# Causal attention from the last tokens to the first, with the mask added to the gate rows on GpSimd

## The chip, the cores and the metric

The kernel runs on one core of one Trainium2 chip. The metric is the device time of one execution in microseconds (us). TensorE (PE) multiplies matrices, VectorE (DVE) and ScalarE (ACT) work on whole tiles, GpSimd (POOL) does some elementwise work and issues some DMAs, SyncE (SP) issues most DMAs. The engines run their own instruction lists in order and wait for each other by semaphores.

## What is computed

One decoder layer on 1024 tokens of width 1024: a projection into four pooling groups and 8 heads of attention with a forget gate, an output projection with layer norm, and an MLP of width 4096 with layer norm. The part that matters here:

```python
log_f = log_sigmoid(f_logit); cf = cumsum(log_f)          # per head
s = (q @ k.T) * HEAD_DIM ** -0.5
s = s + cf[:, None] - cf[None, :]
s = where(kpos <= qpos, s, NEG_INF)                       # causal
p = softmax(s); out = p @ v
x = layer_norm(ALPHA * x + concat([pool_out, out]) @ w_out)
```

The term `cf` of the query drops out of the softmax, so the kernel only adds `-cf` of the keys.

## The kernel before, in words

Matrices are split into a high and a low part (`split`, L70 to L72), and a product takes three passes of TensorE (`three`, L83 to L85). In order of time the program projects values and gates, then three of the four pooling groups, then queries and keys of head pair 0, then runs attention, the output projection with the first norm (from L725, in four pieces `m` of 256 tokens), and the MLP.

Attention (L318 to L443) goes over head pairs `p`, heads `e` of a pair, and pieces `m` of 256 query tokens; one (p, e, m) is a unit. Pairs 0 to 2 run one head after the other with m = 0, 1, 2, 3; pair 3 alternates its two heads for each m. A unit has two halves.

- `att_probs`: for each of its two blocks `i` of 128 queries, and for each piece of up to 512 keys up to the diagonal, two passes give scores in a PSUM bank with the tag "s" (three such banks; L339, L340). If the piece holds the diagonal, a third pass (L342) adds the causal mask, a bf16 identity against a bf16 mask of 128x128. Then DVE's L345 adds the head's gate row, turns the sign and keeps the running minimum, which is the query's maximum; ACT's L347 takes the exponential and the row sum.
- `att_values`: for each 256 keys TensorE transposes the probabilities into a "pt" bank (L368), ACT copies the high part (L369), DVE makes the low part (L370), and TensorE multiplies with the values (L384). The last such tile has a quarter set to zero by POOL (L366). ACT and DVE put the two halves of the result together (L389, L390), and SP writes it to `mix_dram` (L391). `row_scales` turns the row sums into factors (L399 to L404).

The gate row of a head is a line of `ncf_dram` sent to all 128 partitions (L326), into one of the nine buffers of tag "A", where the probabilities and the turned tiles live too. It is asked for by the head's first unit.

`att_values` of a unit is written after `att_probs` of the next one. In between, `fillstep` doles out pieces of other work for TensorE: in pairs 0 to 2 the projection of the next pair's keys and queries (`qk_proj`, 33 pieces over 28 steps), in pair 3 the last pooling group (`pool_group` and `pool_linear`, L242 to L280, 18 pieces over 14 steps). What is left of the pieces runs at the pair's end. A scheduler then sets the order on each engine from this text. The buffers of the token tiles come free as the last pooling group has used them, and take the weights of the output projection, which are split on ACT and DVE inside pair 3.

```python
        prob = att_probs(*unit)
        ...
        fillstep()
        if pend is not None:
            att_values(*pend)
        pend = (*unit, prob)
    run(gen)
```

Of the kernel before, what the change touches and what calls it, by code (L numbers as in the profile page):

```python
# [36 lines left out]
def trunk(ctx, tc, xT, xn, wuqk, wvf, bf, poolw, pscale, wout, g1, b1, w1, w2, g2, b2, out):  # L37
# [13 lines left out]
    def slot(tag, shape, dt=F32R):  # L51
        uid[0] += 1
        return sb.tile([P] + list(shape), dt, tag=tag, bufs=NBUF[tag], name=f"{tag}{uid[0]}")

    def small(shape, tag, dt=F32, bufs=1, pool=None):
        uid[0] += 1
        return (pool or sb).tile(list(shape), dt, tag=tag, bufs=bufs, name=f"{tag}_{uid[0]}")
# [29 lines left out]

    ident = small([P, P], "ident")
    make_identity(nc, ident)
    identb = small([P, P], "identb", BF16)  # L90
    nc.vector.tensor_copy(identb, ident)
    maskb = small([P, P], "maskb", BF16)
    nc.gpsimd.memset(maskb, 0.0)
    nc.gpsimd.affine_select(
        out=maskb, in_=maskb, pattern=[[-1, P]], compare_op=ALU.is_ge,
# [140 lines left out]
    def run(gen):  # L236
        for _ in gen:
            pass
# [51 lines left out]
    def qk_proj(p, tag=None):  # L290
        KS, Q1, Q2 = zip(*([slot("Q", [S]) for _ in range(3)] for _ in range(2)))
        QK[p] = (KS, Q1, Q2)
        lo_, hi_ = slice(0, HD), slice(HD, P)
        w = load_w(wuqk[2 * NPAIR + p])
        for c in range(NCH):
            cs = slice(c * CH, (c + 1) * CH)
            kp = bank(tag)
            for _ in proj(kp, c, w):
                yield
            nc.scalar.copy(KS[0][lo_, cs], kp[lo_])  # L300
            nc.scalar.copy(KS[1][hi_, cs], kp[hi_])
            nc.vector.tensor_tensor(KS[0][hi_, cs], kp[lo_], KS[0][lo_, cs].bitcast(F32), ALU.subtract)
            nc.vector.tensor_tensor(KS[1][lo_, cs], kp[hi_], KS[1][hi_, cs].bitcast(F32), ALU.subtract)
        w = load_w(wuqk[NPAIR + p])
        sc = HD ** -0.5
        for c in range(NCH):
            cs = slice(c * CH, (c + 1) * CH)
            qp = bank(tag)
            for _ in proj(qp, c, w):
                yield  # L310
            for e, r in ((0, lo_), (1, hi_)):
                nc.scalar.mul(Q1[e][r, cs], qp[r], sc)
                nc.vector.scalar_tensor_tensor(Q2[e][r, cs], qp[r], sc, Q1[e][r, cs].bitcast(F32), ALU.mult, ALU.subtract)
            for e, r, o in ((0, lo_, hi_), (1, hi_, lo_)):
                nc.vector.tensor_copy(Q1[e][o, cs], Q1[e][r, cs].bitcast(F32))
                nc.vector.tensor_copy(Q2[e][o, cs], Q2[e][r, cs].bitcast(F32))

    gate_rows, rsum = {}, {}  # L318

    def att_probs(p, e, m):  # L320
        KS, Q1, Q2 = (part[e] for part in QK[p])
        h = 2 * p + e
        if h not in gate_rows:
            gate_rows[h] = slot("A", [S], F32)
            rsum[h] = small([P, NT], "rsum", bufs=3)
            nc.sync.dma_start(gate_rows[h], ncf_dram[h : h + 1, :].to_broadcast([P, S]))  # L326
        nb = gate_rows[h]
        prob = []
        for i in (2 * m, 2 * m + 1):
            nk = (i + 1) * P  # L330
            n2 = nk if m % 2 else 256 * (m + 1)
            qs = slice(i * P, (i + 1) * P)
            pt = slot("A", [S], F32)
            top = BIG
            for a in range(0, nk, CH):
                b = min(n2, a + CH)
                diag = a <= i * P < b
                sp = bank("s")[:, : b - a]
                nc.tensor.matmul(sp, Q1[:, qs], KS[:, a:b], start=True, stop=False)  # L339
                nc.tensor.matmul(sp, Q2[:, qs], KS[:, a:b], start=False, stop=not diag)  # L340
                if diag:
                    nc.tensor.matmul(sp[:, i * P - a : (i + 1) * P - a], identb, maskb, start=False, stop=True)  # L342
                b = min(nk, b)
                nm = small([P, 1], "nm", bufs=8)
                nc.vector.tensor_tensor_reduce(pt[:, a:b], sp[:, : b - a], nb[:, a:b], -1.0, top, ALU.add, ALU.min, nm)  # L345
                top = nm
            nc.scalar.activation(pt[:, :nk], pt[:, :nk], AF.Exp, bias=nm, scale=-1.0, accum_out=rsum[h][:, i : i + 1])  # L347
            prob.append(pt)
        return prob

    def att_values(p, e, m, prob):
        h = 2 * p + e
        rows = slice(e * HD, (e + 1) * HD)
        orow = slice((1 - e) * HD, (2 - e) * HD)
        ov = bank("pv")[:, 0:256]

        def turned(jp):
            tp = bank("pt")
            tt = slot("A", [2, CH])
            if jp < m:  # L360
                blocks = [(jj * 256 + ii * P, 2 * jp + jj, ii) for jj in range(2) for ii in range(2)]
                ev = slice(0, CH)
            else:
                blocks = [(P, 2 * jp + 1, 1), (2 * P, 2 * jp, 0), (3 * P, 2 * jp, 1)]
                ev = slice(P, CH)
                nc.gpsimd.memset(tt[:, :, 0:P].bitcast(F32), 0.0)  # L366
            for col, j, ii in blocks:
                nc.tensor.transpose(tp[:, col : col + P], prob[ii][:, j * P : (j + 1) * P], ident)  # L368
            nc.scalar.copy(tt[:, 0, ev], tp[:, ev])  # L369
            nc.vector.tensor_tensor(tt[:, 1, ev], tp[:, ev], tt[:, 0, ev].bitcast(F32), ALU.subtract)  # L370
            return tt

        nxt = turned(0)
        for jp in range(m + 1):
            tt = nxt
            if jp < m:
                nxt = turned(jp + 1)
            fillstep()
            mov = ((0, 256), (256, CH)) if jp < m else ((256, CH), (0, 256))
            for s in range(2):  # L380
                for jj in range(2):
                    j = 2 * jp + jj
                    a, b = mov[jj]
                    nc.tensor.matmul(  # L384
                        ov, V[j][:, h].rearrange("p s d -> p (s d)"), tt[:, s, a:b],
                        start=(j == 0 and s == 0), stop=(j == 2 * m + 1 and s == 1),
                    )
        mx = slot("U", [256], F32)
        nc.scalar.copy(mx[rows], ov[orow])  # L389
        nc.vector.tensor_tensor(mx[rows], ov[rows], mx[rows], ALU.add)  # L390
        nc.sync.dma_start(mix_dram[m, rows, NG + p, :], mx[rows])  # L391
        if p == NPAIR - 1:
            row_scales(h, 2 * m, 2)
        elif m == 3:
            row_scales(h, 0, NT)

    def row_scales(h, i, n):
        ri = small([P, NT], "ri", bufs=2)
        nc.vector.reciprocal(ri[:, :n], rsum[h][:, i : i + n])  # L399
        tp = bank("pt")  # L400
        nc.tensor.transpose(tp[0:n, 0:P], ri[:, :n], ident)
        row = small([NT, P], "row")
        nc.scalar.copy(row[0:n], tp[0:n, 0:P])
        nc.sync.dma_start(rin_dram[h, i * P : (i + n) * P].rearrange("(i q) -> i q", q=P), row[0:n])  # L404
# [14 lines left out]
    def fillstep():  # L419
        fill["credit"] += fill["rate"]  # L420
        while fill["credit"] >= 1.0:
            fill["credit"] -= 1.0
            next(fill["gen"], None)

    pend = None
    for p in range(NPAIR):
        if p + 1 < NPAIR:
            order = [(p, e, m) for e in range(2) for m in range(4)]
            gen, pieces, over = qk_proj(p + 1, "mm"), 4 * KT + 1, 28
        else:  # L430
            order = [(p, e, m) for m in range(4) for e in range(2)]
            gen, pieces, over = last_fill(), (2 * KT + 2) * len(LATE), 14
        fill.update(gen=gen, credit=0.0, rate=pieces / over)
        for unit in order:
            prob = att_probs(*unit)
            if pend is None:
                for g in EARLY[1:]:
                    pool_linear(g, "A")
            fillstep()
            if pend is not None:  # L440
                att_values(*pend)
            pend = (*unit, prob)
        run(gen)  # L443
    att_values(*pend)


# [275 lines left out]
    NU = NF // 2  # L722
    units = [Unit(u) for u in range(NU)]
    last = None
    for m in range(4):  # L725
        mh = []
        for half in range(2):
            mf = slot("S", [4, 256], F32)
# [7 lines left out]
            hi, lo = slot("Q", [4, 256]), slot("Q", [4, 256])  # L736
            split(hi, lo, mf)
            mh.append((hi, lo))
        for t in (2 * m, 2 * m + 1):
            ts_ = slice((t % 2) * P, (t % 2 + 1) * P)  # L740
            xt = slot("A", [D], F32)
            nc.sync.dma_start(xt, xn[t])
            if t == NT - 1:
                for un in units[:2]:
                    un.load_f()
# [146 lines left out]
    class Step:  # L892
# [61 lines left out]
        def p1(self):  # L954
            self.k1 = bank("s")
            self.prod(self.k1, "A11", "B11", True)
            self.into(0, c0, self.k1, True)
            if self.final:
                self.n0, self.n1 = (Norm(y[t], *rows["gb"], out[t]) for t in (self.q, self.q + 4))

        def p2(self):

# [159 lines left out]
```

## Time and profile before

| | |
|---|---|
| median of 3 runs | 1051.55 us (1051.01 to 1051.81) |
| the profiled execution, its own time | 1053.88 us |
| its span in the profile | 1052.1 us |
| busy: PE, DVE, ACT, POOL | 1021.7, 757.9, 513.1, 116.1 us |
| mask passes (L342) | 64 |
| bytes by DMA | 195.81 MB |

"Busy" is time in which an engine has an instruction at work. Matmuls overlap, so the duration of one is longer than the time between two starts; for what a pass costs, starts are compared. The time in brackets behind a row is how long the engine had been idle before it, with what ended the wait.

### The profile page before, as it was taken

The page shows a single profiled execution, that of the slowest core. Times are in us where ns is not written, and L with a number is a line of the kernel's source. Part 1 is how long each engine was busy: PE and PEld are TensorE (multiplying, and loading weights), DVE is VectorE, ACT ScalarE, POOL GpSimd, SP SyncE. Part 2 cuts the span into 40 slices and gives each one's busy share as a digit, 9 for nine tenths or more (in the row PEclk, how much of TensorE's full clock was granted, in tenths as well). Part 3 has the DMA queues.
Part 4 walks back from the last instruction along what each step waited for, and adds up shares of the span by engine and source line. Part 5 has one row for each costly group of instructions (what it writes and reads, how often), then busy time and mean ns, then how long its engine had stood idle before and what let it go on. Part 6 is the DMA issues. An engine that isn't in the chain of part 4 may idle for free.

```text
span 1052.1 us, 14040 instructions
## 1 busy us (share of the span) xinstructions
PE 1021.7 (97%) x5006; PEld 845.7 (80%) x5006; DVE 757.9 (72%) x1297; ACT 513.1 (49%) x822; POOL 116.1 (11%) x187
## 2 busy tenths in 40 slices
PE   8999999999989999999999999999999999999994
PEld 8988787888777878887888888888788888888883
DVE  4576678686785896989887878788876665566346
ACT  4423565565774331676666766768521212222153
POOL 0000000000000021112112122120100000000056
PEclk9999999999999999999999999999999999999998
DMA  6302311111345633139756667565999888868753
GB/s 221 104 27 93 113 51 32 31 53 50 115 145 169 200 131 110 61 112 349 295 224 266 234 248 271 221 259 195 345 311 300 284 266 279 274 200 276 228 183 120
DMA packets 111654, 195.81 MB, mean 186 GB/s; under 512 B 9240, under 2 KB 77656, under 8 KB 111584
## 3 DMA queue, kind: packets, MB, share of 16 engines
q1 hardware_dynamic: 95600, 136.71, 39.7%
q0 software_dynamic: 15984, 58.20, 14.3%
q8 instruction: 39, 0.64, 0.3%
q14 instruction: 31, 0.25, 0.1%
HBM read 127.18 MB, written 67.70 MB: 185 GB/s over the span
## 4 chain that ended last, share of the span: by engine, by line
PE 52%; DVE 4%; DMA 2%; issue 1%; ACT 0%; DVEq 0%; SPq 0%; ACTq 0%
PE s L932 15%; PE s L578 9%; PE pv L932 8%; PE pt L578 6%; PE mm L578 6%; PE pv L578 4%; PE pt L932 2%; PE mm L932 2%; DMA S<-in_w_dram 1%; DVE B L72 1%; DMA A<-hid_dram 1%; DVE A L701 0%; DVE Q L72 0%; DVE A L516 0%; ACT Q L71 0%
## 5 line engine op out<-in xcount | busy, mean ns | idle before, releaser
L71 ACT CAST B<-S 128x1024 fp32r<-128x1024 f32 (+1 forms) x92 | 78.5, 870 | 178.4 <-DMA S<-in_w_dram 66.5
L72 DVE TENSOR_TENSOR B<-S,B 128x1024 fp32r<-128x1024 f32 (+1 forms) x92 | 90.4, 994 | 39.4 <-ACT B L71 39.1
L578 PE MATMUL s<-B,Q 128*128 128x512 f32 x480 | 113.5, 389 | 0.1
L578 PEld LDWEIGHTS s<-B,Q 128*128 128x128 f32 x480 | 90.0, 188 | 19.2 <-ACT B L71 0.5
L932 PE MATMUL s<-B,Q 128*128 128x512 f32 x399 | 97.2, 390 | 0.0
L932 PEld LDWEIGHTS s<-B,Q 128*128 128x128 f32 x399 | 74.9, 188 | 16.0
L932 PE MATMUL s<-B,A 128*128 128x512 f32 x333 | 83.0, 394 | 3.7 <-DVE rt L499 2.2
L71 ACT CAST Q<-S 128x1024 fp32r<-128x1024 f32 x52 | 54.6, 1050 | 64.3 <-PE s L578 17.0
L932 PEld LDWEIGHTS s<-B,A 128*128 128x128 f32 x333 | 62.3, 188 | 18.9 <-DVE rt L499 2.6
L72 DVE TENSOR_TENSOR Q<-S,Q 128x1024 fp32r<-128x1024 f32 x52 | 63.3, 1216 | 13.8 <-ACT Q L71 13.7
L703 POOL DMA_DIRECT2D hid_dram<-A x90 | 48.2, 540 | 219.6 <-ACT A L700 174.6
L578 PE MATMUL pt<-B,Q 128*128 128x512 f32 x300 | 71.6, 389 | 0.0
L578 PE MATMUL mm<-B,Q 128*128 128x512 f32 x300 | 71.6, 389 | 0.0
L384 PE MATMUL pv<-A,B 128*128 128x256 f32 x320 | 61.9, 298 | 4.8 <-ACT A L369 3.3
L384 PEld LDWEIGHTS pv<-A,B 128*128 128x128 f32 x320 | 49.4, 189 | 21.1 <-ACT A L369 9.7
L578 PEld LDWEIGHTS pt<-B,Q 128*128 128x128 f32 x300 | 56.3, 188 | 11.7
L578 PEld LDWEIGHTS mm<-B,Q 128*128 128x128 f32 x300 | 56.3, 188 | 11.7
L370 DVE TENSOR_TENSOR A<-pt,A 128x512 fp32r<-128x512 f32 (+1 forms) x80 | 49.2, 634 | 16.3 <-ACT A L369 15.7
L347 ACT ACTIVATE A<-A,nm 128x128 f32<-128x128 f32 (+3 forms) x64 | 49.8, 778 | 22.2 <-DVE nm L345 21.9
L701 DVE TENSOR_TENSOR A<-A,A 128x1024 f32<-128x1024 f32 x45 | 53.6, 1219 | 0.0
L83 PE MATMUL mm<-B,B 128*128 128x512 f32 x120 | 51.7, 431 | 0.0
L932 PE MATMUL pv<-B,Q 128*128 128x512 f32 x204 | 50.3, 390 | 0.0
(399 smaller groups left out, 2263.0 us busy)
## 6 DMA issues: line engine op xcount, KB each, us to landing
hid_dram<-A POOLq DMA_DIRECT2D x105, 512.0 KB, 3.9
S<-in_w_dram SPq DMA_DIRECT2D x62, 512.0 KB
Q<-hid_dram SPq DMA_DIRECT2D x104, 256.0 KB
A<-hid_dram SPq DMA_DIRECT2D x76, 256.0 KB
S<-in_wuqk_dram SPq DMA_DIRECT2D x12, 512.0 KB
A<-ncf_dram SPq DMA_DIRECT2D x8, 512.0 KB
S<-in_wout_dram SPq DMA_DIRECT2D x8, 512.0 KB
S<-mix_dram SPq DMA_DIRECT2D x8, 512.0 KB
```

Source lines behind the costliest of these rows:

```text
L71: nc.scalar.copy(hi, src)
L72: nc.vector.tensor_tensor(lo, src, hi.bitcast(F32), ALU.subtract)
L83: nc.tensor.matmul(dst, a[0], b[0], start=first, stop=False)
L347: nc.scalar.activation(pt[:, :nk], pt[:, :nk], AF.Exp, bias=nm, scale=-1.0, accum_out=rsum[h][:, i : i + 1])
L370: nc.vector.tensor_tensor(tt[:, 1, ev], tp[:, ev], tt[:, 0, ev].bitcast(F32), ALU.subtract)
L384: nc.tensor.matmul(ov, V[j][:, h].rearrange("p s d -> p (s d)"), tt[:, s, a:b], start=(j == 0 and s == 0), stop=(j == 2 * m + 1 and s == 1),)
L578: nc.tensor.matmul(dst, b[x][:, k], A[a][y][:, k], start=first and k == 0 and i == 0, stop=k == H - 1 and i == 2, skip_group_check=not first,)
L701: nc.vector.tensor_tensor(x, x, hi.bitcast(F32), ALU.subtract)
L703: nc.gpsimd.dma_start(hid_dram[self.u, :, i, AT[name] : AT[name] + 2 * CH], part.rearrange("p q n t -> p (q n t)"))
L932: nc.tensor.matmul(dst, h[:, p_], w[q_], start=first and u == self.us[0] and j == 0, stop=u == self.us[-1] and j == 2, skip_group_check=no ...
```

## The change

The units run with m = 3, 2, 1, 0, and in each unit the upper block comes first. Before a block's scores, POOL adds the mask, now a float tile, to the 128 columns of the gate row that belong to the block, in place. The blocks above have used these columns without it, and the blocks below don't read them. The mask pass of TensorE, the bf16 identity and its copy go. The gate row of the next unit's head is asked for right after `att_probs` of the current unit. In `qk_proj` the second half of the queries is made first. The output projection takes its four pieces in the order 3, 2, 1, 0, and `PLACE` sends rows to their places in the input and output.

```diff
-    identb = small([P, P], "identb", BF16)
-    nc.vector.tensor_copy(identb, ident)
-    maskb = small([P, P], "maskb", BF16)
+    maskb = small([P, P], "maskb")
...
-        for c in range(NCH):
+        for c in reversed(range(NCH)):
...
+    def gate_row(h):
         if h not in gate_rows:
             gate_rows[h] = slot("A", [S], F32)
             rsum[h] = small([P, NT], "rsum", bufs=3)
             nc.sync.dma_start(gate_rows[h], ncf_dram[h : h + 1, :].to_broadcast([P, S]))
...
-        for i in (2 * m, 2 * m + 1):
+        for i in (2 * m + 1, 2 * m):
             nk = (i + 1) * P
             n2 = nk if m % 2 else 256 * (m + 1)
             qs = slice(i * P, (i + 1) * P)
+            nc.gpsimd.tensor_tensor(nb[:, qs], nb[:, qs], maskb, ALU.add)
...
-                diag = a <= i * P < b
                 sp = bank("s")[:, : b - a]
                 nc.tensor.matmul(sp, Q1[:, qs], KS[:, a:b], start=True, stop=False)
-                nc.tensor.matmul(sp, Q2[:, qs], KS[:, a:b], start=False, stop=not diag)
-                if diag:
-                    nc.tensor.matmul(sp[:, i * P - a : (i + 1) * P - a], identb, maskb, start=False, stop=True)
+                nc.tensor.matmul(sp, Q2[:, qs], KS[:, a:b], start=False, stop=True)
...
-        elif m == 3:
+        elif m == 0:
             row_scales(h, 0, NT)
+    PLACE = [6, 7, 4, 5, 2, 3, 0, 1]
...
+    order = [(p, e, m) for p in range(NPAIR - 1) for e in range(2) for m in (3, 2, 1, 0)]
+    order += [(NPAIR - 1, e, m) for m in (3, 2, 1, 0) for e in range(2)]
...
+        prob = att_probs(*unit)
+        if n + 1 < len(order):
+            gate_row(2 * order[n + 1][0] + order[n + 1][1])
...
-    for m in range(4):
+    for n in range(4):
+        m = 3 - n
...
-            nc.sync.dma_start(xt, xn[t])
+            nc.sync.dma_start(xt, xn[PLACE[t]])
...
-                self.n0, self.n1 = (Norm(y[t], *rows["gb"], out[t]) for t in (self.q, self.q + 4))
+                self.n0, self.n1 = (Norm(y[t], *rows["gb"], out[PLACE[t]]) for t in (self.q, self.q + 4))
```

The order of instructions moves in many places. Three of them follow; the lines of the changed kernel lie a few numbers off (L342 and L343 are there the two score passes, L346 the reduce, L371 the low part of a turned tile, L322 the load of a gate row). The first is TensorE at the start of pair 3, before:

```order
L339 MATMUL s_2876<-Q_2283,Q_2284 128x256
L340 MATMUL s_2876<-Q_2283,Q_2285 128x256
L342 LDWEIGHTS identb_68
L342 MATMUL s_2876<-maskb_70,identb_68 128x128
L339 MATMUL s_2884<-Q_2283,Q_2284 128x256
```

and now:

```order
L342 MATMUL s_2911<-Q_2327,Q_2328 128x512
L343 MATMUL s_2911<-Q_2327,Q_2329 128x512
L342 MATMUL s_2916<-Q_2327,Q_2328 128x512
L343 MATMUL s_2916<-Q_2327,Q_2329 128x512
L342 MATMUL s_2924<-Q_2327,Q_2328 128x512
```

The unit of the first 256 tokens with its two small blocks has made way for the last 256 tokens, whose block takes two banks, and the weight load and the pass of the mask are gone.

The second is VectorE in pair 2, at the two reduces of the unit m = 1 of head 4 (blocks 2 and 3; A_2264 and A_2252 are the gate row), before:

```order
L345 ISA A_2370,nm_2375<-s_2371,A_2264 128x384 [waits DVE_49,PE_49]
L345 ISA nm_2375 128x1
L370 TENSOR_TENSOR A_2323<-pt_2322,A_2323 128x512 [waits Activation_49]
L345 ISA A_2378,nm_2383<-s_2379,A_2264 128x512 [waits DVE_49,PE_49]
L345 ISA nm_2383 128x1
```

and now:

```order
L346 ISA A_2467,nm_2471<-s_2468,A_2252 128x512 [waits DVE_49,PE_49,Pool_49]
L346 ISA nm_2471 128x1
L371 TENSOR_TENSOR A_2423<-pt_2422,A_2423 128x512 [waits Activation_49]
L346 ISA A_2475,nm_2479<-s_2476,A_2252 128x384 [waits PE_49,Pool_49]
L346 ISA nm_2479 128x1
```

Block 3 comes ahead of block 2, and each reduce waits for POOL as well.

The third is the queue of SP around the gate rows of pair 3, before (A_2872 is the row of its first head, A_2976 that of its second):

```order
L326 DMA A_2872<-ncf_dram 128x1024 [waits PE_49,DMAHW0_49,Activation_49,Pool_49]
L391 DMA mix_dram<-U_2868 64x256 [waits DMAHW1_49,DVE_49]
L471 DMA S_3542<-in_wout_dram 128x1024 [waits DMAHW2_49,DVE_49,Activation_49]
L326 DMA A_2976<-ncf_dram 128x1024 [waits DMAHW3_49,DVE_49,PE_49]
L471 DMA S_3546<-in_wout_dram 128x1024 [waits DMAHW4_49,DVE_49]
```

and now (A_2860 and A_2935):

```order
L322 DMA A_2860<-ncf_dram 128x1024 [waits PE_49,DMAHW7_49,Activation_49,Pool_49]
L392 DMA mix_dram<-U_2840 64x256 [waits DMAHW0_49,DVE_49]
L392 DMA mix_dram<-U_2905 64x256 [waits DMAHW1_49,DVE_49]
L408 DMA rin_dram<-row_2972 8x128 [waits DMAHW2_49,Activation_49]
L479 DMA S_3540<-in_wout_dram 128x1024 [waits DMAHW3_49,DVE_49]
L322 DMA A_2935<-ncf_dram 128x1024 [waits DMAHW4_49,PE_49]
L479 DMA S_3544<-in_wout_dram 128x1024 [waits DMAHW5_49,DVE_49]
```

The first head's row stands one write of results further ahead, and the second head's row still stands between two loads of projection weights.

On POOL the new order has, beside the 32 memsets that were there, the 64 adds, most often two to four in a row between two memsets.

## Rows read from the trace of the kernel before

**Rows 1.** The page, busy us (share of the span) and instructions of two engines.

```profile
PE 1021.7 (97%) x5006; PEld 845.7 (80%) x5006; DVE 757.9 (72%) x1297; ACT 513.1 (49%) x822; POOL 116.1 (11%) x187
```

**Rows 2.** Stretches: length, busy us of PE, PEld, DVE, ACT, POOL, clock, DMA share, GB/s.

```profile
111.00:268.70 157.70, 156.32 (x924) 127.08 (x923) 116.17 (x282) 98.75 (x214) 7.19 (x23) 1.00 0.17 54
268.70:295.10 26.40, 24.41 (x145) 19.45 (x144) 21.14 (x49) 19.03 (x44) 1.56 (x5) 1.00 0.40 130
295.10:320.60 25.50, 21.09 (x127) 16.84 (x125) 21.66 (x55) 20.22 (x40) 1.00 (x4) 0.93 0.44 140
320.60:333.40 12.80, 12.22 (x72) 10.44 (x73) 8.98 (x12) 6.07 (x13) 0.24 (x1) 1.00 0.57 151
333.40:1035.00 701.60, 698.25 (x3094) 574.35 (x3093) 515.76 (x735) 325.67 (x438) 93.82 (x125) 1.00 0.67 233
```

**Rows 3.** Timeline of PE at the start of pair 3: start us, us, line, operation.

```profile
268.17 0.71 PE L384 MATMUL pv<-A,B 128*128 128x256 f32 x4
268.72 0.28 PE L339 MATMUL s<-Q,Q 128*128 128x256 f32 x1
268.84 0.28 PE L340 MATMUL s<-Q,Q 128*128 128x256 f32 x1
268.96 0.23 PE L342 MATMUL s<-maskb,identb 128*128 128x128 bf16 x1
269.00 0.36 PE L339 MATMUL s<-Q,Q 128*128 128x256 f32 x1
269.20 0.28 PE L340 MATMUL s<-Q,Q 128*128 128x256 f32 x1
...
269.36 0.48 PE L83 MATMUL mm<-B,B 128*128 128x512 f32 x1
269.67 0.40 PE L84 MATMUL mm<-B,B 128*128 128x512 f32 x1
269.91 0.40 PE L85 MATMUL mm<-B,B 128*128 128x512 f32 x1
270.15 1.04 PE L368 MATMUL pt<-ident,A 128*128 128x128 f32 x8
270.94 0.48 PE L83 MATMUL mm<-B,B 128*128 128x512 f32 x1
271.25 0.40 PE L84 MATMUL mm<-B,B 128*128 128x512 f32 x1
```

**Rows 4.** Groups of instructions in attention: count, busy us, mean ns, idle before.

```profile
L345 DVE CUSTOM_DVE_ANT_0 A<-s,A 128x512 f32<-128x512 f32 x40 | 27.4, 685 | 7.3 <-PE s L340 5.3 <-PE pv L384 1.6 <-issue 0.2
...
L342 PE MATMUL s<-maskb,identb 128*128 128x128 bf16 x64 | 14.8, 231 | 0.0
...
L370 DVE TENSOR_TENSOR A<-pt,A 128x512 fp32r<-128x512 f32 (+1 forms) x80 | 49.2, 634 | 16.3 <-ACT A L369 15.7
```

**Rows 5.** POOL: its memsets as a group, and two adds from its timeline.

```profile
L366 POOL MEMSET A<- 128x256 f32 x32 | 10.0, 312 | 308.6 <-DVE Q L313 112.4 <-PE pv L384 111.9 <-PE pt L368 44.1
...
426.20 1.30 POOL L571 TENSOR_TENSOR A<-A,Q 128x512 f32<-128x512 f32 x1 [12.31 <-DVE Q L567]
437.96 2.74 POOL L571 TENSOR_TENSOR A<-A,Q 128x512 f32<-128x512 f32 x1 [10.46 <-DVE Q L567]
```

**Rows 6.** Timelines of ACT and PE where the output projection starts.

```profile
319.58 1.04 ACT L71 CAST Q<-S 128x1024 fp32r<-128x1024 f32 x1
...
320.67 0.50 PE L83 MATMUL s<-B,Q 128*128 128x512 f32 x1
```

**Rows 7.** Timelines of SP, DVE and PE: the gate row of pair 3's second head.

```profile
275.57 0.33 SPq L326 DMA_DIRECT2D A<-ncf_dram  x1
...
282.78 0.29 DVE L345 CUSTOM_DVE_ANT_0 A<-s,A 128x128 f32<-128x128 f32 x1 [2.00 <-DMA A<-ncf_dram]
...
283.23 0.47 PE L339 MATMUL s<-Q,Q 128*128 128x512 f32 x1 [1.52 <-DVE nm L345]
```

More of the change, by code (lines that the diff above doesn't have):

```diff
@@ L318, in trunk @@
     gate_rows, rsum = {}, {}
-    def att_probs(p, e, m):
-        KS, Q1, Q2 = (part[e] for part in QK[p])
-        h = 2 * p + e
+    def gate_row(h):
         if h not in gate_rows:
@@ L326, in att_probs @@
             nc.sync.dma_start(gate_rows[h], ncf_dram[h : h + 1, :].to_broadcast([P, S]))
+    def att_probs(p, e, m):
+        KS, Q1, Q2 = (part[e] for part in QK[p])
+        h = 2 * p + e
+        gate_row(h)
         nb = gate_rows[h]
         prob = []
-        for i in (2 * m, 2 * m + 1):
+        for i in (2 * m + 1, 2 * m):
             nk = (i + 1) * P
@@ L347, in att_probs @@
             nc.scalar.activation(pt[:, :nk], pt[:, :nk], AF.Exp, bias=nm, scale=-1.0, accum_out=rsum[h][:, i : i + 1])
-            prob.append(pt)
+            prob.insert(0, pt)
         return prob
@@ L423, in fillstep @@
             next(fill["gen"], None)
+    order = [(p, e, m) for p in range(NPAIR - 1) for e in range(2) for m in (3, 2, 1, 0)]
+    order += [(NPAIR - 1, e, m) for m in (3, 2, 1, 0) for e in range(2)]
     pend = None
[L426 to L443, printed above, removed]
+    for n, unit in enumerate(order):
+        p = n // 8
+        if n % 8 == 0:
+            if p + 1 < NPAIR:
+                gen, pieces, over = qk_proj(p + 1, "mm"), 4 * KT + 1, 28
+            else:
+                gen, pieces, over = last_fill(), (2 * KT + 2) * len(LATE), 14
+            fill.update(gen=gen, credit=0.0, rate=pieces / over)
+        prob = att_probs(*unit)
+        if n + 1 < len(order):
+            gate_row(2 * order[n + 1][0] + order[n + 1][1])
+        if pend is None:
+            for g in EARLY[1:]:
+                pool_linear(g, "A")
+        fillstep()
+        if pend is not None:
+            att_values(*pend)
+        pend = (*unit, prob)
+        if n % 8 == 7:
+            run(gen)
     att_values(*pend)
@@ L738, in trunk @@
             mh.append((hi, lo))
-        for t in (2 * m, 2 * m + 1):
+        for t in (2 * n, 2 * n + 1):
             ts_ = slice((t % 2) * P, (t % 2 + 1) * P)
             xt = slot("A", [D], F32)
-            nc.sync.dma_start(xt, xn[t])
+            nc.sync.dma_start(xt, xn[PLACE[t]])
             if t == NT - 1:
```

## Prediction

> **What bounds the kernel now.** I read the busy times first [rows 1]: TensorE (PE) works 1021.7 us, 97% of the span, VectorE (DVE) 757.9. A program that is 97% busy on one engine ends earlier only if that engine loses work or idle time. Then the table by stage [rows 2], where busy time is to be held against length. Attention runs from 111.0 to 333.4 in four stretches: three head pairs, the fourth pair up to its last fill pass, its rest up to the first pass of the output projection, and the piece where both run mixed. PE is idle there for 1.4, 2.0, 4.4 and 0.6 us, 8.4 together. Behind attention, up to 1035.0, it is idle 3.3 of 701.6 us, so what attention gives back should arrive at the end. DVE has 41.5 us free in the 157.7 of the first three pairs, but only 3.8 in the 25.5 of the third stretch, which also has the granted clock at 0.93.
>
> **The mask passes.** 64 of them go, each listed with 231 ns [rows 4]. That is no price, since matmuls overlap; the price is in the starts [rows 3]. A pass of 256 columns starts 0.12 us ahead of the next (268.72, 268.84, 268.96). The mask pass takes 0.04 (268.96 to 269.00), but the pass behind it then takes 0.20 (269.00 to 269.20), and a 512-column one 0.31 (269.36 to 269.67) where its follower takes 0.24. So one costs 0.04 and a slow start of 0.08 behind it. A group of transposes costs the same slow start (270.94 to 271.25), so a mask that stands just ahead of transposes saves less: by the two orders 57 slow starts go. 64 x 0.04 + 57 x 0.08 = **7.1 us**; bounds 2.6 (the 0.04 alone) and 7.7 (64 x 0.12).
>
> **The adds on POOL.** 64 adds of 128x128 come in, which the trace does not have. The nearest rows are a memset of 256 columns, 0.31 us, which reads nothing, and adds of 512 columns, 1.30 at the shortest [rows 5]. A quarter of 1.30 would be 0.33, but part of any instruction doesn't shrink with its columns; I take 0.5, nearest to the scaled row, and keep 0.31 to 1.30. On POOL itself 32 us lie beside 10.0 us of memsets: free. Each memset does queue ahead of adds, but in the new order the DVE step that uses the memset's tile also stands ahead of the reduce that needs the add, so this costs nothing as long as that order holds.
>
> What is not free is the new loop: the add on a block's columns may start only when the reduce of the block above has read them, and the block's own reduce waits for it. 58 of 96 reduces wait for POOL in the new order. For blocks of over 512 columns the first reduce, 0.685 us [rows 4], lies between and hides an add of 0.5. Of the 16 reduces of blocks 2 and 0, six follow their predecessor with nothing between, most others with one step of 0.4 to 0.7. By estimate DVE so waits 6 x 0.5 + 10 x 0.2 = 5 us in all, against 41.5 free: nothing on PE while fill passes stand by. In the stretch without fill five such waits fall on an engine that has 3.8 us to spare: up to 2.5, I take **+1.0 us**; bounds 0 and 6.5 (five at 1.30).
>
> Of two POOL adds of one shape the trace has one at 1.30 us and one at 2.74 [rows 5]: what DVE does beside them can double such an add. The Trainium skill, page "SBUF — State Buffer", section "SBUF: two separate sides", gives this as an exclusive lock: a DVE operation with two SBUF inputs and a GpSimd operation that reads SBUF shut each other out for a whole instruction. By that rule, with which the two rows can agree, the splits of L72 and the adds would delay each other, while the reduces, which read one input from PSUM, would not be touched. The sum goes by the rows: if the five adds that count met a doubled time, 5 x 0.5 more is 2.5 us, which lies within the bounds just given and in rival B.
>
> **The order turned round.** No pass is added. Counted in the orders, between the last fill pass and the first pass of the output projection there were 11264 columns of scores, 40 value passes, 47 transposes, 6 pooling passes and 7 masks; now 7168, 56, 51, 6 and none. By the starts in [rows 3] (0.24 for 512 columns, 0.55 for four value passes, 0.79 for eight transposes) that is 5.3 + 5.5 + 4.6 + 1.4 + 0.8 = 17.6 before and 3.4 + 7.7 + 5.0 + 1.4 = 17.5 now. The stretch took 25.5: 8 us are lost in it. ACT and DVE are busy 20.2 and 21.7 us of it [rows 2]; the pooled group's sums, split and linear pass, its write, the load of the mix and ACT's split at 319.58 must pass through them before the projection starts at 320.67 [rows 6]. All of that stays. Between the same two points the new order has on DVE ten splits of turned tiles (0.63 each, [rows 4]), twelve reduces (from 0.685 for 512 columns, 6 in all), five steps over 1024 columns and four small additions, some 20 us with the POOL waits: about as much as now. The units there are smaller, so less waits on each, but there are more of them. I take **-0.8 us**, bounds -4 (half the loss) and +3 (a loss per unit as now, with five units instead of four).
>
> **The gate rows.** They are asked for one unit earlier. Only one row is waited for today: the second head of the last pair, 2.0 us on DVE and 1.52 on PE [rows 7]; it was issued at 275.57 and used at 282.78, 7.2 us later, among loads of weights. In the new order that load still stands behind a load of out-projection weights on SP, and its reduce comes sooner: by the spacing of the passes ahead of it 6.5 us into the pair, an estimate, instead of 12 (280.8 less 268.7). Issued some 4.5 us into the pair, behind ACT's work that frees SP's queue, it lands near 11.7; DVE then waits about 5, but PE has 4.4 us of fill and value passes in front of the pass that needs the bank, and so waits about 1 instead of 1.5. I cost it at **0**, bounds -1.5 and +2. Each other row's load had no wait and gains nothing. Q's halves change places with the units that need them; the output rows only change addresses; the copy that made the bf16 identity ran before the first matmul mattered.
>
> **Sum.** -7.1 + 1.0 - 0.8 + 0 = -6.9 us. The profiled execution took 1053.88, so it would take 1047.0; the median of the runs, 1051.55, lies 2.33 below it, which gives **1044.6 us**.
>
> **The rivals.** A is this forecast, 1042 to 1047.
>
> B, the waits come back: the loss without fill grows by 2.5, the late gate row by 2, and 7.1 - 4.5 leaves 1049.0. For it: DVE's 3.8 us of room. Against: only 16 of the 64 adds stand where no fill covers them.
>
> C, the short units drain faster: half of the 8 us goes, 1051.55 - 7.1 - 4 = 1040.5. For it: ACT's and DVE's operations there shrink with the columns. Against: the chain through the pooled group is as long as before.
>
> D, slower: the loop through POOL takes over the whole stage. DVE has 41.5 us free for the 48 adds of three pairs, 0.86 each; if every add were exposed by more, hidden by neither a reduce nor another step, DVE would be the bound. At 1.0 each DVE needs 116.2 + 48 = 164.2 for 157.7: +6.5, 1058. For it: 1.30 as the upper bound and the doubled time in [rows 5]. Against: the 0.685 us reduces in between.
>
> E, the passes were free because PE would have waited anyway: 1051. For it: the third stretch. Against: PE idles 1.4 of 157.7 us where 48 of the 64 lie.
>
> **How the numbers follow.** A 0.58, B 0.16, C 0.12, D 0.08, E 0.06. The range, 1040.0 to 1049.6, leaves out D, E and the ends of B and C, some 0.2. A change of under 0.2%, 2.1 us, is about what cannot be told from none; that bound is 1049.4. Faster: A, C and most of B, 0.80; same: E and the rest of B, 0.11; slower 0.09.
>
> **What would show it.** Right: no mask passes; 64 POOL adds near 0.5; the first three pairs about 5 us shorter with PE idle under 3; a fourth pair that still loses some 7 us between fill and projection; DVE waits for POOL of a few us, most in the two smallest units. Wrong: adds above 0.9 us, or PE waiting for banks that DVE frees late (then B or D); a projection that starts within 21 us of the last fill pass (C); a stage as long as before with fewer passes (E).

## The result, and the profile after

The changed kernel takes 1056.25 us (median of 14 runs) against 1050.95 of the kernel before beside it (14 runs). These medians are 5.3 us apart; the ratio of the runs, 1.0043 with a 95% interval of 1.0032 to 1.0054, makes it some 4.5 us slower, and the ratios are used from here on. Forecast was 1044.6, range 1040.0 to 1049.6, with 0.09 for slower. The profiled execution took 1055.57, only 1.7 more than the profiled one of before (1053.88, which is 2.9 above the median of its runs), so the two traces show where time moved, not the whole of the difference.

By stage (columns as in [rows 2], cut at the same places of the program):

```profile
110.20:268.50 158.30, 155.52 (x900) 128.08 (x899) 117.94 (x285) 100.18 (x217) 29.38 (x71) 1.00 0.17 54
268.50:292.80 24.30, 23.16 (x127) 18.93 (x127) 20.38 (x47) 17.61 (x31) 5.60 (x9) 1.00 0.33 115
292.80:319.60 26.80, 21.14 (x134) 17.77 (x132) 22.96 (x56) 21.37 (x49) 8.21 (x15) 0.94 0.44 149
319.60:331.10 11.50, 9.41 (x48) 7.03 (x46) 5.74 (x9) 4.08 (x12) 0.00 (x0) 1.00 0.61 189
331.10:1036.70 705.60, 699.82 (x3093) 575.16 (x3092) 518.11 (x737) 326.64 (x439) 93.72 (x125) 1.00 0.67 232
```

PE has 900 passes in the first three pairs where it had 924: 48 masks went, and 24 came in, 12 value passes and 12 transposes, since the unit still pending at the pair's end is now the smallest one and not the largest. At the spacing of the prediction (0.14 and 0.10) these are 2.9 us, so the stretch should have lost some 5.3 and gained 2.9; it is 0.6 us longer, with PE idle for 2.8 of it where it was 1.4. The stretch without fill grew from 25.5 to 26.8 us with as much PE work as before (21.1) and more on DVE and ACT. What lies behind attention grew from 701.6 to 705.6. The second and the fourth stretch got shorter by 2.1 and 1.3.

The adds on POOL, and two groups that stand beside them (count, busy us, mean ns, idle before):

```profile
L336 POOL TENSOR_TENSOR A<-A,maskb 128x128 f32<-128x128 f32 x64 | 35.7, 558 | 267.1 <-DVE nm L346 165.5
...
L346 DVE CUSTOM_DVE_ANT_0 A<-s,A 128x512 f32<-128x512 f32 x40 | 27.4, 685 | 4.8 <-PE s L343 2.7 <-PE pv L385 1.2 <-PE pt L369 0.7
...
L371 DVE TENSOR_TENSOR A<-pt,A 128x512 fp32r<-128x512 f32 (+1 forms) x80 | 49.0, 634 | 16.5 <-ACT A L370 15.8
```

An add takes 0.56 on average (0.46 as a rule), and DVE's own steps are as long as before [rows 4]. DVE's waits for POOL (us, times, longest), first in the three pairs, then from pair 3 to the projection:

```profile
DVE A L346 <- POOL A L336: 3.9, 8, 0.6
```

```profile
DVE A L346 <- POOL A L336: 0.5, 1, 0.5
```

So 4.4 us on DVE, about as forecast, and only one of these waits in the stretch without cover. The long waits of PE are elsewhere (timeline of PE: start, us, line, operation, idle before and what ended it):

```profile
299.36 0.50 PE L342 MATMUL s<-Q,Q 128*128 128x512 f32 x1 [0.98 <-DVE nm L346]
...
301.47 0.51 PE L385 MATMUL pv<-A,B 128*128 128x256 f32 x2 [0.89 <-ACT A L370]
...
330.29 0.50 PE L83 MATMUL s<-B,Q 128*128 128x512 f32 x1 [2.09 <-ACT Q L71]
...
382.72 0.63 PE L559 MATMUL s<-ident,A 128*128 128x128 f32 x4 [1.00 <-DVE A L524]
...
384.29 0.52 PE L559 MATMUL mm<-ident,A 128*128 128x128 f32 x3 [0.94 <-DVE A L524]
...
486.38 1.22 PE L586 MATMUL pv<-B,Q 128*128 128x512 f32 x2 [2.19 <-DVE A L676]
```

Twice PE then runs at the lower of its two levels, 1.2 GHz (windows, columns as above; the third value from the end is the clock):

```profile
301.80:305.30 3.50, 3.50 (x17) 3.23 (x16) 2.76 (x9) 2.21 (x5) 0.46 (x1) 0.51 0.01 2
486.20:489.60 3.40, 3.22 (x8) 2.54 (x9) 3.37 (x6) 3.11 (x4) 0.35 (x1) 0.50 1.02 405
```

PE is busy nearly throughout such a stretch; 3.4 us at half the clock cost 1.7, by estimate. The first follows two pauses of 0.98 and 0.89 us, the second one of 2.19. The kernel before had one such stretch, in its third row of [rows 2].

### The profile page after: what moved, and what is told of

It is laid out like the page before. It is cut to its first block, busy times and chain, and to the rows that moved or that the text cites. A ratio compares the mean times of both kernels' runs of the same rounds, so it can differ in the third digit from the quotient of the medians.

```text
span 1053.8 us, 13977 instructions
## 1 busy us (share of the span) xinstructions
PE 1017.9 (97%) x4942; PEld 843.9 (80%) x4942; DVE 759.4 (72%) x1296; ACT 513.3 (49%) x822; POOL 150.0 (14%) x251
## 4 chain that ended last, share of the span: by engine, by line
PE 52%; DVE 4%; DMA 2%; issue 1%; ACT 0%; DVEq 0%; SPq 0%; ACTq 0%
PE s L941 15%; PE s L586 9%; PE pv L941 8%; PE pt L586 6%; PE mm L586 6%; PE pv L586 4%; PE pt L941 2%; DMA S<-in_w_dram 2%; PE mm L941 2%; DMA A<-hid_dram 1%; DVE A L709 0%; DVE Q L72 0%; DVE B L72 0%; DVE A L524 0%; ACT Q L71 0%
## 5 line engine op out<-in xcount | busy, mean ns | idle before, releaser
L336 POOL TENSOR_TENSOR A<-A,maskb 128x128 f32<-128x128 f32 x64 | 35.7, 558 | 267.1 <-DVE nm L346 165.5
L385 PE MATMUL pv<-A,B 128*128 128x256 f32 x320 | 64.9, 303 | 7.0 <-ACT A L370 3.2
L371 DVE TENSOR_TENSOR A<-pt,A 128x512 fp32r<-128x512 f32 (+1 forms) x80 | 49.0, 634 | 16.5 <-ACT A L370 15.8
L348 ACT ACTIVATE A<-A,nm 128x1024 f32<-128x1024 f32 (+3 forms) x64 | 49.7, 777 | 20.2 <-DVE nm L346 19.1
L370 ACT CAST A<-pt 128x512 fp32r<-128x512 f32 (+1 forms) x80 | 41.5, 539 | 19.7 <-PE pt L369 18.5
```

What stands on the lines that cost most here:

```text
L336: nc.gpsimd.tensor_tensor(nb[:, qs], nb[:, qs], maskb, ALU.add)
L385: nc.tensor.matmul(ov, V[j][:, h].rearrange("p s d -> p (s d)"), tt[:, s, a:b], start=(j == 0 and s == 0), stop=(j == 2 * m + 1 and s == 1),)
```

## The experiments

All ratios are to the kernel before on the same chip; 0.1% is 1.05 us. Places are read from each run's timeline of PE, in us from the first score pass to the first, the 49th and the last (384th) pass of the output projection and to the end; the last column counts the half-clock stretches between the first score pass and 1035 us (windows of 20 us with a clock under 1). Each row of places is one execution, and not always a typical one: those of e3, e7, e15 and e18 are the shortest runs of their kernels, 1.9 to 2.5 us under the medians.

| kernel | ratio (95%) | first | 49th | last | end | half clock |
|---|---|---|---|---|---|---|
| before | 1 | 209.6 | 226.3 | 308.8 | 941.0 | 1 |
| e1 before again | 0.9997 (0.9988, 1.0007) | 206.0 | 223.0 | 305.5 | 938.7 | 0 |
| e4 old order, no mask | 0.9966 (0.9955, 0.9977) | 198.6 | 217.2 | 300.3 | 933.8 | 0 |
| e2 new order, PE masks | 1.0026 (1.0012, 1.0041) | 210.5 | 224.6 | 309.8 | 941.9 | 1 |
| e3 new order, no mask | 1.0015 (1.0007, 1.0024) | 208.0 | 221.9 | 306.0 | 938.6 | 0 |
| changed | 1.0043 (1.0032, 1.0054) | 209.4 | 224.8 | 308.7 | 943.5 | 2 |
| e13 changed again | 1.0041 (1.0027, 1.0055) | 208.3 | 225.3 | 308.8 | 943.2 | 2 |
| e8 all adds dead | 1.0015 (1.0006, 1.0024) | 208.4 | 222.3 | 306.1 | 941.0 | 1 |
| e14 dead in three pairs | 1.0045 (1.0033, 1.0058) | 208.0 | 223.3 | 307.6 | 941.6 | 0 |
| e15 dead in pair 3 | 1.0015 (1.0003, 1.0026) | 208.6 | 222.6 | 306.2 | 938.4 | 0 |
| e5 changed, 8 steps | 1.0002 (0.9992, 1.0013) | 200.7 | 219.4 | 303.4 | 938.0 | 1 |
| e12 8 steps, adds dead | 0.9986 (0.9973, 0.9998) | 204.9 | 221.8 | 304.4 | 937.6 | 1 |
| e10 before, 8 steps | 1.0001 (0.9986, 1.0016) | 197.9 | 224.1 | 305.4 | 937.3 | 0 |
| e6 three pairs turned | 0.9978 (0.9968, 0.9989) | 205.0 | 221.5 | 303.4 | 934.8 | 0 |
| e11 the same, 8 steps | 0.9974 (0.9960, 0.9989) | 196.7 | 220.8 | 303.7 | 934.7 | 0 |
| e7 scales on POOL's queue | 1.0035 (1.0022, 1.0048) | 209.5 | 222.3 | 305.8 | 939.0 | 0 |
| e9 both | 1.0036 (1.0023, 1.0048) | 200.1 | 227.5 | 308.8 | 943.3 | 4 |
| e16 first scales early | 1.0048 (1.0030, 1.0066) | 213.6 | 226.0 | 309.0 | 943.6 | 2 |
| e17 the same, 8 steps | 1.0014 (1.0001, 1.0027) | 204.6 | 220.7 | 305.6 | 940.7 | 1 |
| e18 early, dead in pair 3 | 1.0047 (1.0032, 1.0063) | 214.3 | 226.2 | 309.8 | 942.3 | 1 |

**Order against mask (e1 to e4).** e1 is the kernel before. e2 puts the mask passes back into the changed kernel, e3 only takes the adds out, e4 takes the passes out of the kernel before:

```diff
# e2, on the changed kernel
-            nc.gpsimd.tensor_tensor(nb[:, qs], nb[:, qs], maskb, ALU.add)
+                if diag:
+                    nc.tensor.matmul(sp[:, i * P - a : (i + 1) * P - a], identb, maskb, start=False, stop=True)
# e3, on the changed kernel
-            nc.gpsimd.tensor_tensor(nb[:, qs], nb[:, qs], maskb, ALU.add)
# e4, on the kernel before
-                if diag:
-                    nc.tensor.matmul(sp[:, i * P - a : (i + 1) * P - a], identb, maskb, start=False, stop=True)
```

> The kernel before once more, unchanged, for the granted clock of each of its runs. Theory CLOCK (part of the difference is that TensorE falls to its lower level more often in the changed kernel, 1.71 us each time in the two traces): the runs differ among themselves by about 1 us for 0.001 of mean clock, and the median clock lies 0.002 or more above the 0.993 of the changed kernel. Rival (the clock has no part in it): the same clock, 0.993, and times that do not follow it.

> The new order with the 64 mask passes back on TensorE and no adds on POOL. Theory ORDER (the turned order alone costs the time, and the passes are worth about 5 us in it): slower than the changed kernel, 1060 to 1062. Theory ADDS (the waits for POOL give back what the passes brought): about the kernel before, 1050 to 1052. Theory FREE (the passes cost nothing because another engine sets the pace): as the changed kernel, 1055 to 1057.

> The changed kernel without the 64 adds: no causal mask at all, everything else kept. Theory ADDS: 5 us or more faster than the changed kernel, 1046 to 1051. Theory ORDER: the adds cost nothing, 1055 to 1057. Theory FREE: as ORDER here.

> The kernel before without its 64 mask passes: no causal mask at all, the old order kept. Theories ORDER and ADDS (a pass costs 0.08 to 0.11 us of TensorE that nothing hides): 5 to 7 us faster than before, 1044 to 1046. Theory FREE (what attention gives back is taken away by a wait behind it): 1049 to 1051, with the gain still to be seen at the first pass of the output projection and gone by 490 us.

1051.23, 1054.13, 1053.20 and 1047.85 us; e2, e3 and e4 lie outside every range expected of them. In the old order the passes are worth 0.34%, 3.6 us (2.4 to 4.7), in the new one about 1 (e2 less e3), which the intervals don't tell from none. The order by itself costs 2.7 us with the passes and 5.1 without them (1.0015 less 0.9966). Adds against nothing cost 3 more. Windows of e4, then of e3 (columns as above), the three pairs first and then from pair 3 to the 49th pass of the projection:

```profile
111.00:264.40 153.40, 151.80 (x876) 125.21 (x876) 115.95 (x282) 99.10 (x214) 7.20 (x23) 1.00 0.18 56
264.40:328.20 63.80, 58.92 (x344) 47.39 (x343) 53.11 (x117) 45.28 (x94) 2.82 (x9) 1.00 0.51 159
```

```profile
110.60:268.20 157.60, 156.03 (x899) 128.28 (x899) 116.20 (x285) 99.96 (x217) 7.58 (x24) 1.00 0.17 54
268.20:332.50 64.30, 56.50 (x320) 45.50 (x320) 50.72 (x113) 43.19 (x91) 2.43 (x8) 1.00 0.48 151
```

In e4 the 48 passes give back 4.3 of 157.7 us, 0.09 each. None of the three theories held alone: ORDER has the largest part, ADDS a second one, and e4 lies between FREE and the other two: the gain is there at the projection, and part of it is gone at the end. CLOCK as I had put it is not borne out by e1: its median clock is 0.994, not 0.995 or more, and its 11 runs hardly follow their mean clock (correlation -0.17). Most of what that mean has lost lies in the closing norm, where PE works 1.5 of 12.3 us (1038.6 to the end in e1's trace). The 14 runs of the changed kernel do follow it, by 0.86 us for 0.001 (correlation -0.71). So the clock has a part in their scatter, and by that slope the 0.001 between the two medians is worth some 0.9 us, an estimate.

**The tail (e5, e6, e10, e11).** e5 hands out the last pooling group's 18 pieces over 8 steps; e10 does so in the kernel before; e6 turns only pairs 0 to 2 and leaves pair 3 and the projection in the old order, with mask passes; e11 is e6 with 8 steps.

```diff
# e5 and e10
-                gen, pieces, over = last_fill(), (2 * KT + 2) * len(LATE), 14
+                gen, pieces, over = last_fill(), (2 * KT + 2) * len(LATE), 8
# e6, on the changed kernel
-        for i in (2 * m + 1, 2 * m):
+        late = p == NPAIR - 1
+        for i in (2 * m, 2 * m + 1) if late else (2 * m + 1, 2 * m):
...
-            nc.gpsimd.tensor_tensor(nb[:, qs], nb[:, qs], maskb, ALU.add)
+            if not late:
+                nc.gpsimd.tensor_tensor(nb[:, qs], nb[:, qs], maskb, ALU.add)
...
-    order += [(NPAIR - 1, e, m) for m in (3, 2, 1, 0) for e in range(2)]
+    order += [(NPAIR - 1, e, m) for m in range(4) for e in range(2)]
```

> The changed kernel with the last pooling group's pieces handed out over 8 steps instead of 14, so that the group is done earlier and its chain to the first output projection starts earlier. Theory TAIL (behind the last fill pass the small units cannot keep TensorE busy, and the projection, which could, starts only when the pooled group has come through): the first projection pass 5 us or more earlier, total 1052 to 1054. Rival (the small units' own work on VectorE and ScalarE sets the end of attention, whatever covers them): within 1 us of the changed kernel, 1055 to 1057.

> Only head pairs 0 to 2 turned round with adds on POOL; pair 3 and the projection in the old order with mask passes on TensorE (the mask tile is bf16 for both). Theory TAIL (the loss is in pair 3 and behind it): faster than before by what three pairs gain, 1048.5 to 1050.5. Theory PAIRS (the waits for POOL and the turned units cost in every pair): as before or slower, 1052 to 1055.

> The kernel before with the pieces over 8 steps instead of 14. Theory TAIL (the early end of the fill matters because the turned order leaves the small units last): here the large units stand last and can cover the chain, so 1050.5 to 1052.5, no gain. Rival (8 steps are better in either order, and say nothing on the turned order): 1047 to 1049.5, as much gain as the 4.5 us of the changed kernel, or most of it.

> Three pairs turned, pair 3 in the old order (1049.1), with the pieces over 8 steps. Theory TAIL: 1048.5 to 1050, nothing more to gain. Rival (8 steps better in either order): 1045 to 1047.5.

1051.70, 1049.12, 1051.38 and 1049.35. The turned kernel gains 4.3 us (1.0043 to 1.0002) from the early group, the kernel before nothing (1.0001), e6 nothing either: what is cured belongs to pair 3 turned round. In e5's timeline of PE the projection comes in at 312.67, among value passes of the small units:

```profile
312.67 0.48 PE L83 MATMUL mm<-B,Q 128*128 128x512 f32 x1
312.99 0.42 PE L385 MATMUL pv<-A,B 128*128 128x256 f32 x2
```

This is 200.7 us behind the first score pass, where it was 209.4, and the 49th pass is 5.4 earlier. In e10 the first pass is 8 us earlier than in e1 and the 49th 1.1 later: the large units that stand last there have work for PE of their own. e6 beats both kernels, the one before by 0.22% (0.11 to 0.32).

**Where the adds cost (e8, e12 to e15).** Dead adds read the same row but write onto the mask tile, so that no one waits; e8 has all of them dead, e14 those of pairs 0 to 2, e15 those of pair 3, e12 is e8 with 8 steps, e13 the changed kernel itself.

```diff
# e8; in e14 only for p < NPAIR - 1, in e15 only for p == NPAIR - 1
-            nc.gpsimd.tensor_tensor(nb[:, qs], nb[:, qs], maskb, ALU.add)
+            nc.gpsimd.tensor_tensor(maskb, nb[:, qs], maskb, ALU.add)
```

> The changed kernel with each add written onto the mask tile instead of the gate row: the same 64 operations on POOL reading the same data, but no VectorE step waits for them (no causal mask in the result). Theory WAITS (the 3 us between the changed kernel and the one without adds are VectorE waiting for POOL): 1052.5 to 1054, as without adds. Theory PORT (they come from POOL and VectorE slowing each other on SBUF): 1055.5 to 1057, as the changed kernel.

> The changed kernel with 8 steps and with the adds written onto the mask tile, so that nobody waits for them (no causal mask in the result). If the waits for POOL cost only where no fill covers the small units: within 1 us of the same kernel with true adds (1051.7), 1050.7 to 1052. If they cost in every pair: 3 us less, 1048 to 1049.5.

> The changed kernel once more, beside the next two on the same chip. If the 3.7 us between it and the kernel with dead adds (1052.5) hold: 1055.5 to 1057. If they were partly the difference of chips and hours, and the traces' 1 us is right: 1053 to 1054.5.

> The changed kernel with the 48 adds of pairs 0 to 2 written onto the mask tile, where nobody waits for them, and the 16 of pair 3 as they are (no true mask in the result). If the waits count in the covered pairs, where the trace has 3.9 of VectorE's 4.4 us: faster than the changed kernel by most of the difference, 1052.5 to 1054. If they count only where no fill covers them: as the changed kernel beside it, within 1 us.

> The other half: the 16 adds of pair 3 written onto the mask tile, the 48 of pairs 0 to 2 as they are. If the waits count only where no fill covers them: faster than the changed kernel by most of the difference, 1052.5 to 1054. If they count in the covered pairs: as the changed kernel beside it, within 1 us.

1052.52, 1050.82, 1056.65, 1056.53 and 1052.89. With 8 steps dead adds bring 0.9 us by the medians, within what was expected if they cost only without cover, but 1.7 by the ratios, whose intervals overlap (e12 against e5): undecided. The work on POOL costs nothing that can be measured (e8 is e3), and neither do the 3.9 us that DVE waits in the covered pairs (e14 is e13). All 3 us lie with the 16 adds of pair 3, where DVE waits 0.5. Beside that wait the scheduler's order differs there. SP's timeline of the changed kernel, and then of e15:

```profile
317.63 0.66 SPq L743 DMA_DIRECT2D S<-rin_dram  x1
320.34 0.25 SPq L408 DMA_DIRECT2D rin_dram<-row  x1
321.39 0.48 SPq L392 DMA_DIRECT2D mix_dram<-U  x1
321.92 0.62 SPq L743 DMA_DIRECT2D S<-rin_dram  x1
```

```profile
317.09 0.66 SPq L743 DMA_DIRECT2D S<-rin_dram  x1
320.00 0.25 SPq L408 DMA_DIRECT2D rin_dram<-row  x1
320.31 0.60 SPq L743 DMA_DIRECT2D S<-rin_dram  x1
321.06 2.48 SPq L392 DMA_DIRECT2D mix_dram<-U  x2
```

The second load of the row scales stands behind one more write in the changed kernel, and PE's pause at the fourth tile is 2.09 us (330.29, above) where e15 has 0.74:

```profile
327.70 0.51 PE L83 MATMUL s<-B,Q 128*128 128x512 f32 x1 [0.74 <-ACT Q L71]
```

That is 1.35 us. The rest, some 1.5, is not placed. Half-clock stretches, two, two and none in the changed kernel, e13 and e14, and none, one and none in e15, e8 and e3, can't be all of it, as e14 is as slow as e13 without one; in its trace PE waits 2.37 us at 760.39 for a load of `hid_dram`, where e15 waits 0.98.

The waits for POOL in pair 3 are not it by themselves. All 16 adds lie ahead of the projection, and its first pass comes 208.3 us behind the first score pass in e13 and 208.0 in e14, with live adds in pair 3, and 208.6 and 208.4 in e15 and e8, with dead ones; none of the four has a half-clock stretch before it.

**The queue (e7, e9, e16 to e18).** e7 issues the loads of the scales from POOL's queue, e9 does so with 8 steps. e16 loads the first piece's scales ahead of the values of the last two units, into a buffer of tag "Q"; e17 is e16 with 8 steps, e18 e16 with pair 3's adds dead (order on PE and SP as in e16).

```diff
# e7 and e9
-                    nc.sync.dma_start(rb[e * HD : (e + 1) * HD], rows.to_broadcast([HD, NPAIR, 256]))
+                    nc.gpsimd.dma_start(rb[e * HD : (e + 1) * HD], rows.to_broadcast([HD, NPAIR, 256]))
# e16 to e18: the same lines moved into scales(m)
+        if n == len(order) - 1:
+            first_scales = scales(3)
```

> The changed kernel with the loads of the row scales (S<-rin_dram) issued from POOL's queue instead of SP's. Theory QUEUE (2.1 us of PE idle at the first piece and 2 us at the second piece's transposes come from these loads standing in SP's queue behind writes that wait): 2 to 4 us faster than the changed kernel, 1052 to 1054. Rival (the loads are late because of the rows or the transfers themselves): 1055.5 to 1057.

> The changed kernel with both edits: the last group's pieces over 8 steps, and the loads of the row scales on POOL's queue. Theory QUEUE (those loads, stuck in SP's queue, cost 1 to 2 us of their own): 1049.5 to 1051, faster than with the 8 steps alone (1051.7). Rival (with the projection started early the loads are in time anyway): 1051 to 1052.5.

> The changed kernel, adds as they are, with the row scales of the first projection piece loaded ahead of the last unit's queries into a buffer of their own. If the place of that one load in SP's queue is what the 3.7 us hang on: no wait of 2.1 us at the first projection's fourth tile, and 1052 to 1053.5. If they hang on the waits of VectorE for POOL themselves: 1055 to 1057, as the changed kernel.

> The same with the last pooling group's pieces over 8 steps. If the two losses (the projection that starts late, the scales that come late) are apart from each other: 1049 to 1051, as the kernel before or faster by 1 to 2 us. If the early projection needs no early scales: 1051 to 1052.5, as with 8 steps alone (1051.7).

> The first of these three with the 16 adds of pair 3 written onto the mask tile, so that nobody waits for them (no true mask there). If the place of the load was all: within 1 us of e16. If the waits for POOL in pair 3 cost by themselves: 2 us or more faster than e16.

1055.02, 1056.15, 1057.13, 1054.46 and 1057.60. e7 is undecided (its interval overlaps that of the changed kernel, and 1055.02 lies between its two ranges), though in its trace PE has no pause at the fourth tile. e9 and e17 lie outside both expectations (e17 by its time; by its ratio, 1.0014, it is near the second one, as the kernel before beside it took 1052.55), e16 is as slow as its rival had it, and e18 is within 1 us of e16. e9 lost all that e5 had won. Its second load lands late, in DVE's order it stands ahead of a split that a value pass needs, and that pass stands ahead of the projection's on PE (DVE's row, then PE's):

```profile
331.39 1.22 DVE L744 TENSOR_TENSOR S<-S,S 128x1024 f32<-128x1024 f32 x1 [3.46 <-DMA S<-rin_dram]
```

```profile
333.26 0.50 PE L385 MATMUL pv<-A,B 128*128 128x256 f32 x2 [3.23 <-DVE A L371]
```

In e16 the pause of 2.09 is gone, but SP now has the norm's rows ahead of the load of the mix, which goes out at 317.45 where it was 314.18, and the projection begins at 324.68 instead of 319.70:

```profile
314.01 0.54 SPq L494 DMA_DIRECT2D Q<-in_g_dram  x1
...
315.89 0.36 SPq L494 DMA_DIRECT2D Q<-in_b_dram  x1
...
317.45 0.58 SPq L747 DMA_DIRECT2D S<-mix_dram  x1
```

e18, with the same order on PE and SP and no one waiting for pair 3's adds, is as slow, so in e16's order too the waits for POOL cost nothing that can be measured. That order loses 4 to 5 us ahead of the projection in another way, so e16 does not tell what the place of the load costs in the changed kernel. That the 3 us are the place of that one load is not shown. What is shown is that they come with live adds in pair 3, that the order of PE, SP, DVE and ACT around the projection changes with them, and that nothing of them is lost before the projection.

## Why the prediction was wrong

**The mask passes: right, but not to the end.** At the 49th projection pass e4 is ahead of e1 by 5.8 us and of the profiled run before by 9.1, of which 1.7 are its half-clock stretch, so 5.8 to 7.4 where 7.1 was forecast. At the end of their traces 4.9 of the 5.8 are left, and 3.6 by the ratio. The sentence that failed is "what attention gives back should arrive at the end": 3.3 us of idle time behind attention were read as room, but DVE's norm and the MLP's weights keep their pace there, and a PE that comes earlier waits for them (0.94 us at 376.66 in e4, and 2.05 at 478.65 where e1 has 1.25 at 485.11).

**The order turned round: the step that failed.** It was put at -0.8, bounds -4 and +3. Without masks it costs 5.1 us, with the mask passes on PE 2.7. By e3 against e4, with 2.9 of work moved out of pair 3 into the three pairs, the traces give 1.3 in the three pairs (157.6 less 153.4 and 2.9), 3.4 from there to the 49th pass (64.3 less 63.8, and 2.9) and 1.0 to the last. The 1.3 are not waiting: PE idles 1.6 us in the three pairs of either, and works 4.2 longer for the passes moved there, which the spacing prices at 2.9; why is open. Of the 3.4, 2.9 are idle time (7.8 against 4.9). The 1.0 are pauses of PE at 380.41 and 381.97 in e3 (0.95 and 0.93), where e4 has one (0.94).

The counts of passes were right (17.5 against 17.6, and PE was busy 21.1 us in both traces), but the step asked what PE has to do and not what covers it. The fill goes by steps, and large units have more steps: turned round, its 14 steps are used up by the fourth unit (before, by the fifth), in the units that have work enough, and four short units (m = 1 and 0) are left with little else between their scores, exponential, transposes and values. Their pauses of 0.6 to 1.05 us each stand in every trace of the new order with 14 steps. The old order has a few as long (0.76 to 1.13 in e1), so it is the sum that tells: from pair 3 to the 49th pass PE idles 8.9 us in the changed kernel and 4.0 in e5, whose edit deals the fill out otherwise. With the mask passes on PE the two orders idle alike there (5.3 in e2, 5.4 in e1). So in the turned pair 3 the passes filled time in which PE would have waited, as rival E had it; this agrees with their being worth about 1 us there. Rival C (short units drain faster) was the contrary of what came. No rival had an order that is slower by itself.

**The adds: size right, price in another place.** 0.46 to 0.56 us each against 0.5; 4.4 us of DVE's waits against 5. While fill stands by, nothing was forecast on PE, and no run tells e14 from e13; in the traces PE idles 2.0 us in the three pairs with dead adds there (e8, e12, e14) and 2.6 to 2.8 with live ones, so some 0.7 by estimate. The +1.0 for pair 3 came as 3, not through those waits but with an order in which SP's queue serves the projection's loads later; 1.35 of it is seen there, the rest stays open. Rival D, the loop through POOL, did not occur.

**The gate row.** Forecast was that PE would wait about 1 us instead of 1.52 [rows 7], put at 0. In the trace after, the row of the second head is issued at 274.82, POOL's add at 279.34 waits 1.50 us for it, and PE not at all. This is no gain that can be booked: e1, the kernel before once more, has no such wait either, so the wait that the prediction read was one of a single execution. No run tried the early load alone.

**Sum.** -3.6 for the passes, +5.1 for the order, +3 for what comes with the adds: +4.5, as measured. This must come out, as the three are differences between the same runs; and they don't add in any order, since the passes are worth 3.6 in the old order and about 1 in the new one.

Half-clock stretches are part of these figures: 16 in the 14 profiles with pair 3 turned, one in the six with pair 3 in the old order, so by estimate (1.14 less 0.17) x 1.7 = 1.7 us between the two groups. Which pause brings one and which does not stays open; e14 has the same pauses as e13 and none.

## What to carry to other kernels

Counting the work that an order gives the busy engine is not enough: ask at each point of the new order what other work stands ready to cover the short chains, and whether the filler is dealt out by steps that the order makes longer or shorter. The price of removed work holds up to the next place where another engine keeps the pace, so follow the saving to the end before booking it. A good part of a change can be had without its bad part (e6): turn round only where filler is to be had.

## What was not expected of the hardware

The prediction allowed for an add of twice the time. Six of the 64 adds, five of them in pair 3, took three times as long, 1.37 to 1.38 us instead of 0.46, each begun some 0.16 us after the start of a DVE step over 1024 columns with two inputs. DVE's and POOL's rows of one of them in the changed kernel, with a plain add:

```profile
305.47 1.22 DVE L72 TENSOR_TENSOR Q<-Q,Q 128x1024 fp32r<-128x1024 f32 x1
```

```profile
304.07 0.46 POOL L336 TENSOR_TENSOR A<-A,maskb 128x128 f32<-128x128 f32 x1 [2.46 <-DVE nm L346]
305.63 1.37 POOL L336 TENSOR_TENSOR A<-A,maskb 128x128 f32<-128x128 f32 x1 [1.10 <-DVE nm L346]
```

DVE's step ends at 306.69 in its usual 1.22 us, the add at 307.00: it ended only when DVE was through. The Trainium skill, page "SBUF — State Buffer", section "SBUF: two separate sides", states this as an exclusive lock for a whole instruction; these rows agree, with DVE as the one that came first. As nothing of the 3 us is lost ahead of the projection, where these adds stand, no cost of it is seen here.
